# Low parts of split weights: a ScalarE copy with a negative sign and an accumulating DMA from GpSimd, in place of a VectorE subtraction

## The chip, the cores and the metric

The program runs on one core of a Trainium2 chip. The metric is the device time of one execution in microseconds; it is the median of three runs where several are given. The core has five engines, each with an instruction queue of its own that runs in order: TensorE (PE; its weight loads are PEld), VectorE (DVE), ScalarE (ACT), GpSimd (POOL) and SyncE (SP). SP issues most of the DMAs, GpSimd the rest; 16 DMA engines carry them.

## What is computed

Two blocks of a language model at sequence length 512 and width 1024, all in float32. The first has a convolution layer and a sliding-window layer, each followed by a feed-forward network; the second has compressed, selected and windowed attention beside a retention, then a gated merge. Nearly all of the arithmetic is in products of activations with weights:

```python
h = rmsnorm(x, norm_ffn[i])
x = x + (jax.nn.silu(h @ w_gate[i]) * (h @ w_up[i])) @ w_down[i]
...
y_b = (o_b * jax.nn.silu(z_r)) @ w_ret_o
merged = jax.nn.sigmoid(m_a) * y_a + jax.nn.sigmoid(m_b) * y_b
x = x + rms_norm(merged @ w_out, norm_post)
```

## The kernel before

Float32 products are made from three products in the format fp32r, which keeps fewer bits: each operand is split into a high part (the value rounded to fp32r) and a low part (what is left), and high x high, high x low and low x high are summed in PSUM. The names in the profile end in h and l for the two parts: `wh`, `wl` for weights, `gh`, `gl` and others for activations.

`weights` (L93) loads one weight tile of 128 x 1024 (512 KB; 896 columns in two thirds of the down projections, 512 in `w_nsa_o`, 1120 in `w_in_vg`) into `wr` by a DMA on SP (L102), copies it rounded into `wh` on ScalarE (L65, `copy`), and subtracts `wh` from `wr` into `wl` on VectorE (L75, `lo_of`). This happens 278 times. Only the first two tiles come in halves (`parts=2`), so that there are 280 copies and 280 subtractions. The buffers rotate: two `wr`, three `wh`, three `wl`. A load therefore waits until the tile two before it has been read for the last time, and a copy until TensorE is done with the tile three before it.

Two functions use the tiles. `proj` (L117) makes one 128 x 512 output from one tile: for each chunk of 128 rows, three matmuls (L111 to L113) of 512 columns, 24 for a tile of eight chunks, and the tile is free after that. `proj_tok` (L124) holds two tiles at once, of four chunks each, and goes through both for each block of 128 tokens (L133 to L135), so that both come free only in the last block.

The order of instructions on each engine is set when the program is built, by a scheduler that goes through the code in program order and puts each engine's instructions in a static queue. Semaphores do the rest. GpSimd's queue holds elementwise work too: the product `u` x `z` of each feed-forward column (L68), the squares and sums of the norms (L148, L157), clears of value tiles, and its own DMA issues.

Of the kernel before, what the change touches and what calls it, by code (L numbers as in the profile page):

```python
# [8 lines left out]
F32 = mybir.dt.float32  # L9
# [3 lines left out]
ALU = mybir.AluOpType  # L13
# [14 lines left out]
class Build:  # L28
# [65 lines left out]
    def weights(self, src, nk, nn, parts=1):  # L94

        nc, n = self.nc, nk * nn
        raw = self.wp.tile([128, 1120], F32, name=self.nm("wr"), tag="wr", bufs=self.wbufs["wr"])
        hi = self.wp.tile([128, WMAX], F32R, name=self.nm("wh"), tag="wh", bufs=self.wbufs["wh"])
        lo = self.wp.tile([128, WMAX], F32R, name=self.nm("wl"), tag="wl", bufs=self.wbufs["wl"])
        step = n // parts  # L100
        for s in (slice(a, a + step) for a in range(0, n, step)):
            nc.sync.dma_start(raw[:, s], src[:, s] if parts > 1 else src)  # L102
        for s in (slice(a, a + step) for a in range(0, n, step)):
            self.copy(hi[:, s], raw[:, s])
            self.lo_of(lo[:, s], raw[:, s], hi[:, s])
        v = lambda t: t[:, :n].rearrange("p (k c) -> p k c", k=nk)
        return v(hi), v(lo)

# [1017 lines left out]
```

## Time and profile before

| | us |
|---|---|
| median of three runs (1670.31 to 1672.84) | 1670.35 |
| the profiled execution's own time | 1670.48 |
| its span, first to last instruction | 1668.7 |
| TensorE busy in it | 1634.9 |
| VectorE busy | 1059.2 |
| ScalarE busy | 639.0 |
| GpSimd busy | 247.1 |
| SP's DMA queue, as busy time of all 16 DMA engines (27.3% of the span) | 455.6 |

The span is what the trace covers; the execution's own time is 1.8 us longer. TensorE's granted clock is full (a mean of 0.995) for nearly the whole span. Busy shares of TensorE overlap in the pipeline: a matmul of 512 columns shows 0.39 us, and the next one starts 0.23 us after it.

### The profile page before, as it was taken

What the parts mean: (1) busy time and instruction counts of PE and PEld (TensorE: products, weight loads), DVE (VectorE), ACT (ScalarE), POOL (GpSimd) and SP (SyncE); (2) the same over time, 40 slices, a digit from 0 to 9 for tenths busy, and PEclk for the clock granted to TensorE, in tenths of its full rate; (3) what the DMA queues carried; (4) which work ended last, traced back from release to release, by engine and by line L of the source; (5) the groups of instructions that cost most, each with busy time, mean ns of one, the idle gap of its engine ahead of it and who ended that gap; (6) DMA issues with size and microseconds to landing.
All of it is one profiled execution on the core that took longest, in us unless ns stands there. A gap on an engine that the chain in (4) does not pass through costs nothing.

```text
span 1668.7 us, 21221 instructions
## 1 busy us (share of the span) xinstructions
PE 1634.9 (98%) x8184; PEld 1374.2 (82%) x8184; DVE 1059.2 (63%) x1828; ACT 639.0 (38%) x1134; POOL 247.1 (15%) x220
## 2 busy tenths in 40 slices
PE   8999999999999999999999999998999999999997
PEld 6888888888888788888888888878788888888887
DVE  7776745444454979875434435588788977764443
ACT  5532333222333467633222223324465533333333
POOL 1111411002011600051100101351001000010010
PEclk9999999999999999999999999999999999999999
DMA  5323222322352422122332332332401122243342
GB/s 188 118 85 102 91 98 91 101 101 85 118 160 91 159 83 84 62 102 88 101 101 95 100 109 91 101 138 93 166 28 58 45 82 83 70 151 114 126 159 88
DMA packets 51557, 171.39 MB, mean 103 GB/s; under 512 B 6680, under 2 KB 6880, under 8 KB 51328
## 3 DMA queue, kind: packets, MB, share of 16 engines
q1 hardware_dynamic: 45504, 151.11, 27.3%
q0 software_dynamic: 5376, 18.82, 3.4%
q8 instruction: 64, 1.05, 0.2%
q14 instruction: 37, 0.30, 0.1%
q10 hardware_dynamic: 576, 0.11, 0.0%
HBM read 160.56 MB, written 11.81 MB: 103 GB/s over the span
## 4 chain that ended last, share of the span: by engine, by line
PE 82%; DVE 10%; issue 2%; ACT 2%; DMA 1%; POOL 1%; DVEq 0%; SPq 0%; ACTq 0%; POOLq 0%
PE pp L112 11%; PE pp L113 11%; PE pp L111 11%; PE lg L111 8%; PE lg L112 8%; PE lg L113 7%; PE tp L112 3%; PE tp L253 2%; PE tp L113 2%; PE tp L111 2%; DVE wl L75 2%; PE po L111 2%; PE po L112 2%; PE po L113 2%; PE pp L133 2%
## 5 line engine op out<-in xcount | busy, mean ns | idle before, releaser
L65 ACT ACTIVATE wh<-wr 128x1024 fp32r<-128x1024 f32 (+2 forms) x280 | 288.5, 1030 | 695.1 <-PE pp L112 228.0
L75 DVE TENSOR_TENSOR wl<-wr,wh 128x1024 fp32r<-128x1024 f32 (+2 forms) x280 | 388.7, 1389 | 55.5 <-ACT wh L65 52.3
L111 PE MATMUL pp<-gh,wh 128*128 128x512 f32 x880 | 348.0, 396 | 7.4 <-ACT wh L65 5.9
L113 PE MATMUL pp<-gh,wl 128*128 128x512 f32 x880 | 347.2, 395 | 0.6 <-DVE wl L75 0.6
L112 PE MATMUL pp<-gl,wh 128*128 128x512 f32 x880 | 346.7, 394 | 0.5 <-DVE gl L71 0.5
L111 PEld LDWEIGHTS pp<-gh,wh 128*128 128x128 f32 x880 | 166.7, 190 | 41.4 <-ACT wh L65 6.4
L113 PEld LDWEIGHTS pp<-gh,wl 128*128 128x128 f32 x880 | 166.4, 189 | 33.9 <-DVE wl L75 1.6
L112 PEld LDWEIGHTS pp<-gl,wh 128*128 128x128 f32 x880 | 166.6, 189 | 33.2 <-DVE gl L71 1.3
L111 PE MATMUL lg<-gh,wh 128*128 128x512 f32 x408 | 159.8, 392 | 0.0
L112 PE MATMUL lg<-gl,wh 128*128 128x512 f32 x408 | 159.1, 390 | 0.0
L113 PE MATMUL lg<-gh,wl 128*128 128x512 f32 x408 | 158.8, 389 | 0.0
L68 POOL TENSOR_TENSOR u<-u,z 128x512 f32<-128x512 f32 x44 | 64.8, 1472 | 549.7 <-DVE u L68 432.6
L68 DVE TENSOR_TENSOR u<-lg,Rf 128x512 f32<-128x512 f32 x44 | 30.4, 691 | 137.4 <-PE lg L113 137.3
L112 PEld LDWEIGHTS lg<-gl,wh 128*128 128x128 f32 x408 | 76.7, 188 | 16.5 <-issue 0.7
L111 PEld LDWEIGHTS lg<-gh,wh 128*128 128x128 f32 x408 | 76.6, 188 | 16.3 <-issue 0.5
L113 PEld LDWEIGHTS lg<-gh,wl 128*128 128x128 f32 x408 | 76.6, 188 | 16.1 <-issue 0.2
L112 PE MATMUL tp<-actl,wh 128*128 128x512 f32 x216 | 84.5, 391 | 0.9 <-DVE actl L75 0.9
L111 PE MATMUL tp<-acth,wh 128*128 128x512 f32 x216 | 84.1, 389 | 0.0
L113 PE MATMUL tp<-acth,wl 128*128 128x512 f32 x216 | 84.1, 389 | 0.0
L68 DVE TENSOR_TENSOR z<-pp,Rf 128x512 f32<-128x512 f32 x44 | 30.4, 691 | 69.5 <-PE pp L113 65.7
L504 DVE TENSOR_TENSOR x<-x,tp 128x512 f32<-128x512 f32 x36 | 24.6, 683 | 65.5 <-PE tp L113 65.5
L71 DVE SCALAR_TENSOR_TENSOR gl<-x,gains,gh 128x512 fp32r<-128x512 f32 x40 | 52.9, 1338 | 0.5 <-ACT gh L65 0.5
(422 smaller groups left out, 3088.9 us busy)
## 6 DMA issues: line engine op xcount, KB each, us to landing
wr<-in_w_gate_dram SPq DMA_DIRECT2D x44, 512.0 KB, 3.2
wr<-in_w_up_dram SPq DMA_DIRECT2D x44, 512.0 KB, 3.2
wr<-in_w_in_dram SPq DMA_DIRECT2D x44, 512.0 KB, 3.2
wr<-in_w_down_dram SPq DMA_DIRECT2D x32, 448.0 KB, 3.3
wr<-in_a_w_in_dram SPq DMA_DIRECT2D x18, 512.0 KB, 3.2
wr<-in_w_down_dram SPq DMA_DIRECT2D x16, 512.0 KB, 3.5
wr<-in_a_w_out_dram SPq DMA_DIRECT2D x8, 512.0 KB, 3.2
wr<-in_b_w_q_dram SPq DMA_DIRECT2D x8, 512.0 KB, 3.2
```

Of the source, the lines that this page charges most:

```text
L65: self.nc.scalar.activation(out, in_, AF.Copy, scale=scale)
L68: (eng or self.nc.vector).tensor_tensor(out, a, b, op=ALU.mult)
L71: (eng or self.nc.vector).scalar_tensor_tensor(out, a, s, b, op0=op0, op1=op1)
L75: self.nc.vector.tensor_tensor(out, x, hi.bitcast(F32), op=ALU.subtract)
L111: mm(ps, ah, bh, start=start, stop=False)
L112: mm(ps, ah, bl, start=False, stop=False)
L113: mm(ps, al, bh, start=False, stop=stop)
L133: mm(ps, a, wh, start=k == 0, stop=False)
L253: self.nc.tensor.transpose(ps[:, c:c + 128], src, self.ident)
L504: nc.vector.tensor_tensor(self.x[c], self.x[c], ps, op=ALU.add)
```

## The change

For every tile that is loaded whole, the subtraction on VectorE goes. ScalarE makes a second copy with scale -1 into `wl`, which leaves the rounded high part there with its sign turned, and a DMA issued by GpSimd then adds the raw tile to it in place (`accum_op=ALU.add`), reading `wr` and `wl` in SBUF and writing `wl`. The result is the same low part, not rounded again to fp32r. The two first tiles, in halves, keep the subtraction.

```diff
--- before.py
+++ after.py
@@ -102,7 +102,11 @@
             nc.sync.dma_start(raw[:, s], src[:, s] if parts > 1 else src)
         for s in (slice(a, a + step) for a in range(0, n, step)):
             self.copy(hi[:, s], raw[:, s])
-            self.lo_of(lo[:, s], raw[:, s], hi[:, s])
+            if parts > 1:
+                self.lo_of(lo[:, s], raw[:, s], hi[:, s])
+            else:
+                self.copy(lo[:, s], raw[:, s], -1.0)
+                nc.gpsimd.dma_start(lo[:, s].bitcast(F32), raw[:, s], accum_op=ALU.add)
         v = lambda t: t[:, :n].rearrange("p (k c) -> p k c", k=nk)
         return v(hi), v(lo)
```

With it, the `wr` buffer is read for the last time by the DMA, and no longer by VectorE: the next load into that buffer waits for the end of the DMA. TensorE's L113 waits for the DMA. SP's queue keeps its 316 entries in the same order but for small exchanges at two places. Lines after L104 have numbers higher by 4 in the changed kernel.

GpSimd's queue in the first feed-forward block, where before it holds only the products `u` x `z`:

```order
L68 TENSOR_TENSOR u_1825<-u_1825,z_1791 128x512
L68 TENSOR_TENSOR u_1897<-u_1897,z_1863 128x512
L68 TENSOR_TENSOR u_1969<-u_1969,z_1935 128x512
L68 TENSOR_TENSOR u_2041<-u_2041,z_2007 128x512
L68 TENSOR_TENSOR u_2113<-u_2113,z_2079 128x512
```

and now:

```order
L68 TENSOR_TENSOR u_1857<-u_1857,z_1822 128x512
L109 DMA wl_1941<-wr_1939 128x1024
L109 DMA wl_1976<-wr_1974 128x1024
L68 TENSOR_TENSOR u_1931<-u_1931,z_1896 128x512
L109 DMA wl_2015<-wr_2013 128x1024
L109 DMA wl_2050<-wr_2048 128x1024
L68 TENSOR_TENSOR u_2005<-u_2005,z_1970 128x512
L109 DMA wl_2089<-wr_2087 128x1024
L109 DMA wl_2124<-wr_2122 128x1024
```

Two issues stand between each product and the next; the product of one column stands ahead of the issue for the next column's gate tile.

ScalarE's queue at the same place, before (`wh` copies, the Silu of `z`, the high part of the product):

```order
L65 ACTIVATE wh_1940<-wr_1939 128x1024
L493 ACTIVATE z_1863<-z_1863 128x512
L65 ACTIVATE wh_1978<-wr_1977 128x1024
L65 ACTIVATE acth_1900<-u_1897 128x512
L65 ACTIVATE wh_2012<-wr_2011 128x1024
L493 ACTIVATE z_1935<-z_1935 128x512
```

and now:

```order
L65 ACTIVATE wh_1940<-wr_1939 128x1024
L65 ACTIVATE acth_1860<-u_1857 128x512
L65 ACTIVATE wl_1941<-wr_1939 128x1024
L65 ACTIVATE wh_1975<-wr_1974 128x1024
L65 ACTIVATE wl_1976<-wr_1974 128x1024
L497 ACTIVATE z_1896<-z_1896 128x512
L65 ACTIVATE wh_2014<-wr_2013 128x1024
L65 ACTIVATE wl_2015<-wr_2013 128x1024
```

Each `wh` copy has a `wl` copy of the same tile behind it, with at one place the high part of a product in between.

GpSimd's queue in the residual that feeds the first feed-forward norm, where it squares and sums the new `x` chunks, before:

```order
L148 TENSOR_TENSOR acc_1734<-x_81 128x512
L148 TENSOR_TENSOR sq_1736<-x_82 128x512
L157 TENSOR_TENSOR acc_1734<-acc_1734,sq_1736 128x512
L148 TENSOR_TENSOR sq_1739<-x_83 128x512
L157 TENSOR_TENSOR acc_1734<-acc_1734,sq_1739 128x512
```

and now:

```order
L109 DMA wl_1506<-wr_1504 128x1024
L152 TENSOR_TENSOR acc_1765<-x_81 128x512
L109 DMA wl_1539<-wr_1537 128x1024
L152 TENSOR_TENSOR sq_1767<-x_82 128x512
L161 TENSOR_TENSOR acc_1765<-acc_1765,sq_1767 128x512
L109 DMA wl_1572<-wr_1570 128x1024
L152 TENSOR_TENSOR sq_1770<-x_83 128x512
L161 TENSOR_TENSOR acc_1765<-acc_1765,sq_1770 128x512
```

One issue stands between each pair of a square and a sum and the next pair, so that the issue waits behind both, and behind what the square waits for.

## Rows read from the trace of the kernel before

**Rows 1.** The page: busy us, share and instructions of each engine
```profile
PE 1634.9 (98%) x8184; PEld 1374.2 (82%) x8184; DVE 1059.2 (63%) x1828; ACT 639.0 (38%) x1134; POOL 247.1 (15%) x220
```

**Rows 2.** The chain that ended last, its shares by line
```profile
by line: PE pp L112 11.4%; PE pp L113 11.4%; PE pp L111 11.3%; PE lg L111 7.6%; PE lg L112 7.6%; PE lg L113 7.5%; PE tp L112 2.5%; issue 2.5%; PE tp L253 2.5%; PE tp L113 2.4%; PE tp L111 2.4%; DVE wl L75 2.2%; PE po L111 2.2%; PE po L112 1
```

**Rows 3.** Groups by line: busy us, mean ns, idle before and its releasers
```profile
L75 DVE TENSOR_TENSOR wl<-wr,wh 128x1024 fp32r<-128x1024 f32 (+2 forms) x280 | 388.7, 1389 | 55.5 <-ACT wh L65 52.3
...
L65 ACT ACTIVATE wh<-wr 128x1024 fp32r<-128x1024 f32 (+2 forms) x280 | 288.5, 1030 | 695.1 <-PE pp L112 228.0 <-PE lg L112 196.4 <-PE tp L112 98.1
```

**Rows 4.** Timeline, first feed-forward block: start us, us, engine, line, operation
```profile
250.09 1.06 ACT L65 ACTIVATE wh<-wr 128x1024 fp32r<-128x1024 f32 x1 [2.44 <-PE pp L112]
...
251.18 1.22 DVE L75 TENSOR_TENSOR wl<-wr,wh 128x1024 fp32r<-128x1024 f32 x1 [0.22 <-ACT wh L65]
...
252.43 0.33 SPq L102 DMA_DIRECT2D wr<-in_w_up_dram  x1
...
255.53 1.06 ACT L65 ACTIVATE wh<-wr 128x1024 fp32r<-128x1024 f32 x1 [3.86 <-PE lg L112]
...
256.56 1.29 POOL L68 TENSOR_TENSOR u<-u,z 128x512 f32<-128x512 f32 x1 [9.59 <-DVE u L68]
256.62 2.32 DVE L75 TENSOR_TENSOR wl<-wr,wh 128x1024 fp32r<-128x1024 f32 x1 [0.23 <-ACT wh L65]
...
260.94 0.39 PE L111 MATMUL lg<-gh,wh 128*128 128x512 f32 x1
...
260.97 1.06 ACT L65 ACTIVATE wh<-wr 128x1024 fp32r<-128x1024 f32 x1 [2.44 <-PE pp L112]
```

**Rows 5.** DMA queues: packets, MB, share of 16 engines
```profile
q1 hardware_dynamic: 45504, 151.11, 27.3%
```

**Rows 6.** DMA issues: count, KB each, median us to landing
```profile
wr<-in_w_gate_dram SPq DMA_DIRECT2D x44, 512.0 KB, 3.2
...
wr<-in_w_down_dram SPq DMA_DIRECT2D x32, 448.0 KB, 3.3
...
band<-band POOLq DMA_DIRECT2D x1, 2304.0 KB, 13.8
...
wr<-in_w_nsa_o_dram SPq DMA_DIRECT2D x8, 256.0 KB, 2.8
...
xt<-xt POOLq DMA_DIRECT2D x8, 256.0 KB, 2.5
```

**Rows 7.** The same, issues from 541 to 549 us only
```profile
xres<-x POOLq DMA_DIRECT2D x2, 256.0 KB, 2.3
```

**Rows 8.** The same, issues from 552 to 560 us only
```profile
xres<-x POOLq DMA_DIRECT2D x2, 256.0 KB, 3.9
```

**Rows 9.** GpSimd from 541 to 560 us: one issue
```profile
542.26 0.59 POOL L514 DMA_DIRECT2D xres<-x  x1
```

**Rows 10.** ScalarE, 421 to 440 us, down projection of seven chunks
```profile
422.58 0.96 ACT L65 ACTIVATE wh<-wr 128x896 fp32r<-128x896 f32 x1 [3.80 <-PE po L112]
427.34 0.96 ACT L65 ACTIVATE wh<-wr 128x896 fp32r<-128x896 f32 x1 [3.80 <-PE tp L112]
```

**Rows 11.** ScalarE, 1154 to 1190 us, compression weights: first, one, last
```profile
1154.59 1.05 ACT L65 ACTIVATE wh<-wr 128x1024 fp32r<-128x1024 f32 x1
...
1167.68 1.06 ACT L65 ACTIVATE wh<-wr 128x1024 fp32r<-128x1024 f32 x1 [3.64 <-DMA wr<-in_w_in_dram]
...
1187.17 1.06 ACT L65 ACTIVATE wh<-wr 128x1024 fp32r<-128x1024 f32 x1 [0.19 <-DMA wr<-in_w_in_dram]
```

**Rows 12.** ScalarE, 1633 to 1638 us, output projection
```profile
1634.96 1.06 ACT L65 ACTIVATE wh<-wr 128x1024 fp32r<-128x1024 f32 x1 [0.78 <-PE pp L134]
1636.40 1.06 ACT L65 ACTIVATE wh<-wr 128x1024 fp32r<-128x1024 f32 x1 [0.38 <-PE pp L134]
```

**Rows 13.** Groups by line, GpSimd
```profile
L157 POOL TENSOR_TENSOR acc<-acc,sq 128x512 f32<-128x512 f32 x24 | 40.9, 1705 | 1.1
```

**Rows 14.** Windows, busy us of instructions with wl: PE, PEld, DVE
```profile
1122.00:1190.00 68.00, 36.38 (x109) 19.00 (x108) 19.81 (x15) 0.97 0.35 117
```

## The prediction

> **What bounds the kernel now.** I read the busy times first [rows 1]: TensorE is busy for 1634.9 us of 1668.7, so only 33.8 us of the span have no matmul at all. The chain that ended last, by line [rows 2], is matmul lines almost throughout; VectorE's low parts of weights (wl L75) hold 2.2% of it, 36.7 us. That is the most that this line's wait can be worth. The groups by line [rows 3] show the two steps of a weight tile: the copies on ScalarE cost 288.5 us in all, 1.03 us each, and before them ScalarE sits idle for 695.1 us, mostly until a matmul frees a buffer; the subtractions cost VectorE 388.7 us, 1.39 us each. Both steps run well ahead of TensorE.
>
> How far ahead, a stretch of the timeline shows [rows 4]. The copy into wh starts at 250.09 when a buffer comes free, the subtraction at 251.18, and the load for the tile after the next is issued at 252.43, as the subtraction ends. The next copies start at 255.53 and 260.97: one tile each 5.44 us, paced by the matmuls (a new tile begins at 260.94). The tile copied at 250.09 is the one used from 260.94, so its low part lies ready for more than 8 us. The two wr buffers give a second limit: two tiles take 10.88 us, and a buffer's own round (load 3.2 us [rows 6], copy 1.06, subtraction 1.22 to 2.32 [rows 4]) is 5.5 to 6.6 us. Here nothing waits for the weights.
>
> **What goes and what comes.** 276 of the 280 subtractions go, about 385 us of VectorE's 1059.2. ScalarE gets 276 copies of the size of wh's, 1.03 us each by [rows 3]: 284 us on 639.0 [rows 1], still 55% of the span. GpSimd gets 276 issues at 0.59 us each, the cost of a plain one [rows 9]: 163 us on 247.1. No engine becomes the bound by its sum. What decides is the wr buffer's round, which now holds a second copy and a whole DMA where a subtraction of 1.22 us was.
>
> **The DMA's time, D, from issue to landing.** No accumulating DMA and none from SBUF to SBUF stands in the trace, so I bound it. GpSimd's writes of 256 KB from SBUF landed in 2.3 us in one stretch [rows 7] and in 3.9 us ten microseconds later [rows 8]; another of its 256 KB copies has 2.5 us [rows 6]. SP's queue moved 151.11 MB in 27.3% of the span [rows 5], 455.6 us, which is 0.332 MB per us: 1.58 us for 512 KB and 0.79 for 256 KB. A plain copy of 512 KB from GpSimd is then 2.3 + 0.79 = 3.1 us. That is the lower bound, with the addition and the read of the old wl for nothing. If that second read goes through the same engines it adds 1.58: 4.7 us. Upper bound: GpSimd's slowest copy, 2304 KB in 13.8 us [rows 6], moves 0.17 MB per us; 512 KB twice at that rate is 6.1 us, and with the 1.5 us of the 2.3 that are not transfer 7.6 us. I take 4.7, since it rests on the quick 256 KB rows at the usual rate and the bytes that must be read.
>
> The Trainium skill speaks to the doubling (Collectives: The Full Stack, section on the bandwidth ceiling): an addition in the DMA path costs no time of its own but needs two source reads on the same ring, and a measured ratio of 1.93 to a plain copy is given. By it the transfer would be 3.05 us and D 4.6; by the plain-copy row alone D is 3.1 and the kernel would be some 1680 us. No run so far shows which holds.
>
> **Tiles of 512 KB in steady state.** The round is load 3.2, two copies 2.12, D 4.7, and 0.2 for hand-offs (at every second tile the issue also stands behind the product u x z, which ends at 257.85 [rows 4], 0.2 us after the second copy would): 10.2 us against 10.88. It hides, with 0.7 us to spare where 4.3 to 5.4 were. But one tile now needs 1.58 + 3.16 = 4.74 us of all 16 DMA engines out of 5.44, and the load into one buffer runs while the other buffer's addition does; each can lengthen the other by up to 1.58. I take 1.0: 11.2 us, an excess of 0.32 per two tiles, 0.16 per tile. Some 130 tiles (gate, up, large down, most of a_w_in and both out projections) have this pattern: 21 us.
>
> **Down projections of seven chunks.** The copies are 4.76 us apart [rows 10], 9.52 for two. The round is 3.3 [rows 6] + 2 x 0.96 + 4.3 (D less an eighth of its transfer) + 0.2 + 0.9 for sharing = 10.6: 0.55 for each of 32 tiles, 18 us.
>
> **Compression weights.** These tiles feed few matmuls, and the kernel already waits for loads here [rows 11]: from the first to the last copy nine steps of 3.62 us, with a wait for a raw tile among them. The new round of 10.2 us gives 5.1 per tile: 9 x 1.48 = 13 us.
>
> **Output projection.** proj_tok holds two of the three buffers, so that the second tile of the next group is copied only when the first of this group comes free, at 1634.96; the other comes free 1.44 us later, at 1636.40 [rows 12]. TensorE then has 1.44 us of the next group's first tile, so that the low part is needed about 3.1 us after 1634.96. Now it is there after 2.12 + 0.2 + 4.7 = 7.0: 3.9 us lost at three joints, 12 us. The eight other proj_tok calls have other tiles between them; each loses something from 0 to 3.9, I take 1.1: 9 us.
>
> **The rest.** In the merge, w_nsa_o tiles of 256 KB (load 2.8 [rows 6], copies 1.1, D 3.1, 0.2: 7.2) alternate with w_ret_o tiles (10.2); the mean of the rounds is 8.7 against 8.16 us of matmuls (5.44 and half of it): 0.5 in each of eight steps, 4 us. Where GpSimd squares and sums, the issue waits behind a square and a sum; a sum is 1.71 us [rows 13] and takes up more than the spare 0.7, and in three norms I count 5 us for both.
>
> **What comes back.** VectorE is relieved where it is on the chain: the subtractions are 19.8 us of the 68 from 1122 on [rows 14], the densest stretch. The 36.7 us of the chain and the 33.8 us without matmuls are ceilings; but in this stretch the subtraction's place is taken by the longer DMA, and ScalarE, which is in every softmax, gets a copy for each tile. I take 8 us.
>
> **Sum.** 21 + 18 + 13 + 12 + 9 + 4 + 5 - 8 = 74 us on the span of 1668.7: 1742.7, and with the 1.8 us outside it 1744.5. The profiled execution's own time, 1670.48, lies 0.13 above the median, so that 1744 stands for the median.
>
> **Rivals.** (1) The DMA is little slower than a plain copy, D from 3.1 to 3.9. The steady round is 8.6 to 9.4 us and hides with its sharing. Left are the joints: output projection 3 x 2.5 = 7, compression 6, the other calls 4, GpSimd's queue 3; less 8: +12, 1682. For it: the quick 256 KB row; against: the old wl must be read.
>
> (2) GpSimd's transfers start late beside a busy VectorE: the same 256 KB took 2.3 and 3.9 us [rows 7, 8]. D is then 6.3, the steady round with sharing 12.8: 0.96 x 130 = 125; seven chunks 1.25 x 32 = 40; the joints, compression and the rest grow by 1.6 us each time, from 43 to about 75. Less 8: +232, 1902. The Trainium skill has a rule for this (SBUF — State Buffer, section on its two separate sides): GpSimd cannot write descriptors while VectorE holds the shared port in a two-port mode. The page gives the plain two-input operation, which was VectorE's commonest, no such mode, so that by the rule D would stay at 4.7 in the feed-forward blocks; rows 7 and 8 do not say which operation held the transfer up.
>
> (3) The addition itself is slow, D near 7.6. The engines are then held so long that loads wait for all of their 1.58 us: the round is 14.7, 1.9 x 130 = 247; seven chunks 2 x 32 = 64; the rest about 90; less 8: +393, 2063.
>
> (4) Faster. If D is near 3.1 and the joints are covered by work that the scheduler moved there, the 36.7 us of low parts on the chain [rows 2] come back by half: -18 and +4, 1656. It decides from D under about 3 us.
>
> **Chances.** The forecast (1700 to 1800) 0.40, (1) 0.15, (2) 0.21, (3) 0.17, (4) 0.07. The forecast's own range is 1705 to 1795. To hold 8 in 10 the range leaves out (4) and the upper half of (3): 1676 to 2060. About 0.2%, 3.3 us, is what a measurement of this kernel can tell from no change. Faster by more has 0.07, within it 0.03 (a part of rival 1), slower 0.90.
>
> **What would show it.** In the changed profile: wl gone from VectorE but for four instructions, ScalarE near 920 us; a row of GpSimd's issues wl<-wr, whose time to landing is D: near 4.7 if the two reads are the cost, 3.1 to 3.9 for rival 1, over 6 for 2 and 3. The first start of L113 should wait for the DMA mainly in the seven-chunk down projections, the compression and the output projection. If the feed-forward copies still start each 5.44 us, sharing was mis-sized and the steady terms of 39 us go; if they start at 6.5 us or more, D was. I am wrong altogether if D is under 3 or over 8 us.

## The result, and the profile after

The changed kernel takes 1928.34 us (median of four runs, 1901.21 to 1952.99), the kernel before 1670.33: the ratio is 1.142, with a 95% interval from 1.135 to 1.150. (The two longest of the four runs are left out of the ratio, which is why it is below 1928/1670.) The profiled execution took 1915.94 us with a span of 1913.8. The forecast was 1744: the direction was right, the size was not. The measured time lies inside the stated range of 1676 to 2060, but outside the forecast's own of 1705 to 1795. On the span 245 us came on where I had summed up 74.

The page of the changed kernel: busy times, GpSimd's DMA queue (packets, MB, share of 16 engines), the chain that ended last, by engine and by line, groups of instructions, and two rows of DMA issues (KB each, median us to landing).

```profile
PE 1711.9 (89%) x8184; PEld 1401.3 (73%) x8184; DVE 686.1 (36%) x1552; ACT 878.1 (46%) x1410; POOL 453.5 (24%) x496
...
q0 software_dynamic: 45120, 159.44, 42.1%
...
DMA 46%; PE 31%; issue 12%; ACT 7%; DVE 2%; POOL 1%; SPq 0%; ACTq 0%; POOLq 0%; DVEq 0%
DMA wl<-wr 24%; DMA wr<-in_w_gate_dram 6%; DMA wr<-in_w_down_dram 4%; ACT wl L65 4%; PE pp L117 4%; PE pp L116 4%; PE pp L115 4%; DMA wr<-in_w_in_dram 3%; DMA wr<-in_w_up_dram 3%; PE tp L257 2%; DMA wr<-in_a_w_in_dram 2%; PE po L115 2%; PE lg L117 1%; PE lg L115 1%; PE po L116 1%
...
L65 ACT ACTIVATE wh<-wr 128x1024 fp32r<-128x1024 f32 (+2 forms) x280 | 287.6, 1027 | 826.9 <-DMA wr<-in_w_down_dram 168.0
L109 POOL DMA_DIRECT2D wl<-wr x276 | 238.8, 865 | 1189.8 <-ACT wl L65 1005.4
L117 PE MATMUL pp<-gh,wl 128*128 128x512 f32 x880 | 356.3, 405 | 33.4 <-DMA wl<-wr 33.3
...
wl<-wr POOLq DMA_DIRECT2D x234, 512.0 KB, 5.0
wr<-in_w_gate_dram SPq DMA_DIRECT2D x44, 512.0 KB, 4.2
```

The chain is no longer made of matmuls [rows 2]: its largest link is the loop of a raw buffer, addition (24%), load, copy. ScalarE's copies into wh waited for matmuls before [rows 3]; now they wait for loads, and the matmuls of L117 (L113 before) wait for the low part. VectorE lost 373 us of work [rows 1], and no gain from it can be seen. The addition's D is 5.0 us in the median, near my 4.7; but the loads, 3.2 before [rows 6], now take 4.2.

That median hides two patterns. The first, from 555 to 576 us, as a timeline (start us, us, engine, line, operation, idle before and its releaser):

```profile
562.08 0.86 POOL L109 DMA_DIRECT2D wl<-wr  x1 [6.09 <-ACT wl L65]
562.18 0.51 PE L117 MATMUL pp<-gh,wl 128*128 128x512 f32 x1 [1.34 <-DMA wl<-wr]
562.19 0.33 SPq L102 DMA_DIRECT2D wr<-in_w_gate_dram  x1
...
566.35 1.06 ACT L65 ACTIVATE wh<-wr 128x1024 fp32r<-128x1024 f32 x1 [4.57 <-DMA wr<-in_w_gate_dram]
...
568.65 0.86 POOL L109 DMA_DIRECT2D wl<-wr  x1 [4.39 <-ACT wl L65]
568.76 0.50 PE L117 MATMUL lg<-gh,wl 128*128 128x512 f32 x1 [0.81 <-DMA wl<-wr]
568.77 0.33 SPq L102 DMA_DIRECT2D wr<-in_w_up_dram  x1
```

Each addition (562.08) is issued 0.1 us ahead of the load for the other buffer (562.19), and so again at 568.65 and 568.77, with two tiles to a round: a buffer is loaded at 562.2 and again at 575.4, 13.2 us later. What the DMA engines do in the 3.3 us that follow the two issues shows in the packets of the queues from 562 to 565.3 us (the last two rows: the issues of this window, us to landing):

```profile
q1 hardware_dynamic: 119, 0.48, 60.4%
q0 software_dynamic: 2, 0.01, 1.2%
...
wl<-wr POOLq DMA_DIRECT2D x1, 512.0 KB, 6.6
wr<-in_w_gate_dram SPq DMA_DIRECT2D x1, 512.0 KB, 4.1
```

The load (q1) moves all but its last packets and the addition (q0), although issued first, next to nothing: the addition does not share with the load, it stands behind it. D is 6.6 there, and TensorE gets a tile each 6.6 us instead of 5.44.

The second pattern, 296 to 313 us:

```profile
296.79 0.87 POOL L109 DMA_DIRECT2D wl<-wr  x1 [4.83 <-ACT wl L65]
...
299.21 0.86 POOL L109 DMA_DIRECT2D wl<-wr  x1 [1.56 <-ACT wl L65]
301.27 0.33 SPq L102 DMA_DIRECT2D wr<-in_w_gate_dram  x1
...
304.23 0.33 SPq L102 DMA_DIRECT2D wr<-in_w_up_dram  x1
...
307.81 0.87 POOL L109 DMA_DIRECT2D wl<-wr  x1 [4.74 <-DMA wr<-in_w_up_dram]
...
310.24 0.86 POOL L109 DMA_DIRECT2D wl<-wr  x1 [1.55 <-ACT wl L65]
312.31 0.33 SPq L102 DMA_DIRECT2D wr<-in_w_down_dram  x1
```

Two additions follow each other in 2.4 us, then both loads; the two additions land in 4.7 us (their median). The round is 312.31 - 301.27 = 11.04 us, almost the 11.2 that I had forecast for everywhere. Here it is the load that waits: it is issued at 301.27, and from 302 to 303.2 us the engines start 61 packets of the additions and none of its own. In both patterns the transfer whose packets come first goes through first. Below, "lockstep" is the first pattern and "pairs" the second.

### The profile page after: what moved, and what is told of

It reads as the page before. It is cut to its first block, busy times and chain, and to the rows that moved or that the text cites. A ratio compares the mean times of both kernels' runs of the same rounds, so it can differ in the third digit from the quotient of the medians.

```text
span 1913.8 us, 21841 instructions
## 1 busy us (share of the span) xinstructions
PE 1711.9 (89%) x8184; PEld 1401.3 (73%) x8184; DVE 686.1 (36%) x1552; ACT 878.1 (46%) x1410; POOL 453.5 (24%) x496
## 3 DMA queue, kind: packets, MB, share of 16 engines
q0 software_dynamic: 45120, 159.44, 42.1%
## 4 chain that ended last, share of the span: by engine, by line
DMA 46%; PE 31%; issue 12%; ACT 7%; DVE 2%; POOL 1%; SPq 0%; ACTq 0%; POOLq 0%; DVEq 0%
DMA wl<-wr 24%; DMA wr<-in_w_gate_dram 6%; DMA wr<-in_w_down_dram 4%; ACT wl L65 4%; PE pp L117 4%; PE pp L116 4%; PE pp L115 4%; DMA wr<-in_w_in_dram 3%; DMA wr<-in_w_up_dram 3%; PE tp L257 2%; DMA wr<-in_a_w_in_dram 2%; PE po L115 2%; PE lg L117 1%; PE lg L115 1%; PE po L116 1%
## 5 line engine op out<-in xcount | busy, mean ns | idle before, releaser
L109 POOL DMA_DIRECT2D wl<-wr x276 | 238.8, 865 | 1189.8 <-ACT wl L65 1005.4
L117 PE MATMUL pp<-gh,wl 128*128 128x512 f32 x880 | 356.3, 405 | 33.4 <-DMA wl<-wr 33.3
L115 PE MATMUL pp<-gh,wh 128*128 128x512 f32 x880 | 354.9, 404 | 20.8 <-ACT wh L65 14.8
L116 PE MATMUL pp<-gl,wh 128*128 128x512 f32 x880 | 352.5, 401 | 0.9 <-DVE gl L71 0.9
L65 ACT ACTIVATE wl<-wr 128x1024 fp32r<-128x1024 f32 (+3 forms) x276 | 281.3, 1019 | 0.6 <-PE pp L117 0.6
L117 PEld LDWEIGHTS pp<-gh,wl 128*128 128x128 f32 x880 | 169.7, 193 | 80.1 <-DMA wl<-wr 46.8
L117 PE MATMUL lg<-gh,wl 128*128 128x512 f32 x408 | 164.0, 402 | 12.0 <-DMA wl<-wr 11.9
L117 PEld LDWEIGHTS lg<-gh,wl 128*128 128x128 f32 x408 | 77.7, 191 | 35.7 <-DMA wl<-wr 19.1
L75 DVE TENSOR_TENSOR actl<-u,acth 128x512 fp32r<-128x512 f32 x36 | 24.9, 693 | 208.5 <-ACT acth L65 208.5
L117 PE MATMUL tp<-acth,wl 128*128 128x512 f32 x216 | 87.0, 403 | 7.5 <-DMA wl<-wr 7.5
L71 DVE SCALAR_TENSOR_TENSOR gl<-x,gains,gh 128x512 fp32r<-128x512 f32 x40 | 39.0, 989 | 95.4 <-ACT gh L65 95.4
```

The source lines that it names most:

```text
L65: self.nc.scalar.activation(out, in_, AF.Copy, scale=scale)
L71: (eng or self.nc.vector).scalar_tensor_tensor(out, a, s, b, op0=op0, op1=op1)
L75: self.nc.vector.tensor_tensor(out, x, hi.bitcast(F32), op=ALU.subtract)
L109: nc.gpsimd.dma_start(lo[:, s].bitcast(F32), raw[:, s], accum_op=ALU.add)
L115: mm(ps, ah, bh, start=start, stop=False)
L116: mm(ps, ah, bl, start=False, stop=False)
```

## The experiments

How long each tile is late is worked out from the traces: the time from the first matmul of one tile to that of the next, less the same time in the kernel before, summed over the tiles that are waited for (in the order of before). In us, with the count of tiles; "changed" is the changed kernel, e1 to e12 the experiments, "mem, kv" the tiles of w_mem_k, w_mem_v, w_kv_k and w_kv_v, "layer a" those of a_w_in and a_w_out:

```
tiles      count  changed       e1       e2       e3       e4       e6       e8      e10      e11      e12
gate, up      88     62.0     11.3     11.6      0.2     12.3     20.5     71.1      5.5     70.0     21.0
down          48     33.6     -2.1      0.7     -2.1     -1.9      4.5     42.8      0.1     21.9      3.7
layer a       28     17.7      0.7      6.9     -0.2      3.2     10.2      3.1     15.0      1.0      6.5
mem, kv       12     33.5     10.9      5.2     -1.9      9.3      4.8      7.7     23.1      8.4      4.8
w_in          44     46.2     14.7     29.1      7.6     17.5      3.4      6.8     44.4      5.4      6.9
cmp_w1         8     21.9     13.0     17.7      1.7     10.9     18.0     -1.6     18.6     -1.9      0.3
w_out          8     17.5     10.0     28.3      0.8     10.4     16.0     -0.0     19.8     -0.0      0.1
w_nsa_o        8      7.9      0.1      0.7      0.0      0.8      0.9     -0.6      9.3      0.0      1.4
the rest      34      1.9      2.9      6.2      0.3     -0.9     -1.8     -0.0      4.4     -0.1      6.3
sum          278    242.3     61.5    106.3      6.5     61.8     76.6    129.2    140.1    104.7     50.9
```

A negative number is a tile that came sooner than before, or other work that the static queues put elsewhere.

My theory, called S in the expectations: loads and additions pass one behind the other, and a raw buffer's round cannot hold both. The rivals: the second read of the addition is not what costs (L), the 16 engines are simply full, or ScalarE's second copy holds up the chain.

**e1, a plain copy in place of the addition.**

```diff
-                nc.gpsimd.dma_start(lo[:, s].bitcast(F32), raw[:, s], accum_op=ALU.add)
+                nc.gpsimd.dma_start(lo[:, s].bitcast(F32), raw[:, s])
```

> The DMA from GpSimd only copies the raw weights over wl and adds nothing (so the low parts hold the whole weight; what is left out is the subtraction of the high part). The waits, the queues and ScalarE's second copy are those of the changed kernel. Theory S (the transfers of loads and additions do not share the 16 engines but pass one behind the other, and the raw buffer's round cannot hold both): a transfer with one read takes about 1.3 to 1.6 us instead of 2.6, D alone 3.1 to 3.4, behind a load about 5; the round is at most 3.2 + 2.1 + 5 + 0.2 = 10.5 of 10.88 us, so the steady loss goes: 1690 to 1735 us. Theory L (what costs is that a DMA from GpSimd starts late and stands in the wait chain, however little it moves): D stays above 4.5, 1850 us or more.

1733.62 us, a ratio of 1.039 (1.037 to 1.041). Its queue of GpSimd and its issues:

```profile
q0 software_dynamic: 42560, 159.44, 23.4%
...
L109 POOL DMA_DIRECT2D wl<-wr x276 | 152.6, 553 | 924.4 <-ACT wl L65 832.1
...
wl<-wr POOLq DMA_DIRECT2D x234, 512.0 KB, 3.1
wr<-in_w_gate_dram SPq DMA_DIRECT2D x44, 512.0 KB, 3.2
```

D is 3.1 us, my lower bound to the digit, and the loads are back at 3.2. Down, layer a and the merge (w_nsa_o) lose nothing more. L falls: the waits and queues are the same and three quarters of the loss are gone. What is left, 61 us, sits where stages meet; 11.6 of it lies in one feed-forward group, which is told below.

**e2, the addition reads HBM, so that wr is free after the two copies.**

```diff
-                nc.gpsimd.dma_start(lo[:, s].bitcast(F32), raw[:, s], accum_op=ALU.add)
+                nc.gpsimd.dma_start(lo[:, s], src.bitcast(F32R), accum_op=ALU.add)
```

> The accumulating DMA reads the raw weights from HBM instead of from wr, so that a raw buffer is free once ScalarE has made its two copies: round 3.2 + 2.1 = 5.3 to 7 us instead of 10 to 13.5. The number and size of the additions stay. Theory S: the raw buffer's round was what held the kernel; D may stay at 4.5 to 7, but a wl buffer has 10.85 us from its copy to its use, of which 2.1 + 7 + 0.2 = 9.3 are used; left are the joints (output projection, compression, the ends of stages): 1700 to 1760 us. Rival (the additions themselves keep the 16 engines too long, whoever waits): the same number of bytes must still be added, over 1860 us.

1781.67 us, 1.067 (1.064 to 1.069), somewhat over the range of S.

```profile
q0 software_dynamic: 45120, 159.44, 48.1%
...
wr<-in_w_gate_dram SPq DMA_DIRECT2D x44, 512.0 KB, 5.2
...
wl<-in_w_gate_dram POOLq DMA_DIRECT2D x44, 512.0 KB, 7.7
```

This is the clearest reading of the study: loads take 5.2 us and additions 7.7, both longer than in the changed kernel, and yet gate, up and down lose 12 us instead of 96. Neither the engines' load nor D itself cost there; the raw buffer that was held for D did. The long D costs where a low part is needed soon: 28 us in the output projection (17.5 in the changed kernel), which I had not counted in. (Both sides are named as fp32r here; the queue moves the same 159.44 MB.)

**e3, the ScalarE part alone.**

```diff
-                nc.gpsimd.dma_start(lo[:, s].bitcast(F32), raw[:, s], accum_op=ALU.add)
+                nc.vector.tensor_tensor(lo[:, s], raw[:, s], lo[:, s].bitcast(F32), op=ALU.add)
```

> ScalarE's negated copy stays, and VectorE adds the raw weights (no DMA): the ScalarE part of the change alone. All theories that blame the DMA: within 10 us of the kernel before, 1665 to 1682. Rival (the second copy on ScalarE, in front of the copies of act and z, holds up the chain): 1720 us or more.

1677.3 us, 1.0044 (1.0029 to 1.0059). The 276 copies cost some 7 us by themselves. ScalarE's work is not the cause; that the order of its queue passes a late load on is told below.

**e4, half of each tile by the DMA.**

```diff
-                self.copy(lo[:, s], raw[:, s], -1.0)
-                nc.gpsimd.dma_start(lo[:, s].bitcast(F32), raw[:, s], accum_op=ALU.add)
+                h = slice(0, n // 2)
+                self.copy(lo[:, h], raw[:, h], -1.0)
+                nc.gpsimd.dma_start(lo[:, h].bitcast(F32), raw[:, h], accum_op=ALU.add)
+                h = slice(n // 2, n)
+                self.lo_of(lo[:, h], raw[:, h], hi[:, h])
```

> Only the left half of each tile goes by ScalarE's negated copy and the accumulating DMA; VectorE subtracts the right half as before. Theory S: D alone is 1.43 + 1.3 + 0.35 = 3.1 us, behind a load 5; the round is 3.2 + 1.6 + 5 + 0.2 = 10 at most, under 10.88: 1690 to 1730 us, a third or less of the loss although half of the bytes stay. Rival (each added byte costs its share, wherever it lies): half of the 258 us stays, about 1800. Theory L (a late start of each DMA, whatever its size): over 1850.

1734.16 us, 1.039 (1.037 to 1.040), just over the range of S: a quarter of the loss for half of the bytes. D is 3.3 us for 256 KB. True additions that are short enough for the round cost about what the plain copies of e1 cost: every row of the table is within 4 us.

**e5 and e6, a third raw buffer.** There is no room in SBUF for one, so some was given up elsewhere first (e5), and then used (e6).

```diff
-WMAX = 1152
+WMAX = 1120
-        self.sm = pool("sm", 4)
+        self.sm = pool("sm", 3)
-    def square_sum(self, chunks, n=512, first=False, gain2=None, tags=("sa", "s")):
+    def square_sum(self, chunks, n=512, first=False, gain2=None, tags=("s", "s")):
-        self.const("pad", [128, 88])
...
-        self.wbufs = dict(wr=2, wh=3, wl=3)
+        self.wbufs = dict(wr=3, wh=3, wl=3)
```

(In the slots' counts sa=1 goes and k3=2 becomes k3=1. The last pair of lines is e6 alone.)

> The changed kernel with some SBUF given up elsewhere (one buffer less for small tiles and the last keys, the sums of squares in the slots of the squares, wh and wl 1120 wide), and nothing put in its place: the control of the next run. All theories: the time of the changed kernel, 1900 to 1955 us.

> The control with a third raw buffer in the space given up. Theory S (a raw buffer's round of load, two copies and addition cannot hold a load and an addition that pass one behind the other): three buffers may take 16.3 us for their round, and 4.5 + 2.1 + 7 + 0.2 = 13.8 fits even where every addition waits behind a load; the loss of the gate, up, down and a-layer tiles (113 us by the traces) goes but for 20, the joints stay: 1730 to 1790 us. Rival (the 16 engines are the bound, or additions are too slow whoever waits): within 40 us of the control.

1953.15 us for e5 (1.169, 1.162 to 1.176), 25 us above the changed kernel's median and at the upper end of its four runs; 1750.58 for e6 (1.0485, 1.0469 to 1.0500).

```profile
wl<-wr POOLq DMA_DIRECT2D x234, 512.0 KB, 5.8
wr<-in_w_gate_dram SPq DMA_DIRECT2D x44, 512.0 KB, 5.1
```

As in e2, additions and loads are slower than in the changed kernel, and the buffer that makes room for them takes back 203 us against the control and 178 against the changed kernel. For that part the engines are not the bound.

**e7, no loads.** In front of the tiles one raw tile is loaded; only the first two tiles, which go in two parts, have a load of their own.

```diff
-        raw = self.wp.tile([128, 1120], F32, name=self.nm("wr"), tag="wr", bufs=self.wbufs["wr"])
+        raw = self.raw0 if parts == 1 else self.wp.tile([128, 1120], F32, name=self.nm("wr"), tag="wr", bufs=1)
...
-        for s in (slice(a, a + step) for a in range(0, n, step)):
+        for s in (slice(a, a + step) for a in range(0, n if parts > 1 else 0, step)):
             nc.sync.dma_start(raw[:, s], src[:, s] if parts > 1 else src)
```

> All weight tiles but the first two are made from one raw tile that is loaded once (left out: the other 278 loads; all tiles hold the same weights). The copies, the additions and their waits stay; no load runs beside an addition and no raw buffer is waited for. Theory S: D is 4.4 to 5.0 us throughout, never 6 to 8 except behind another addition; steady loss nil, the joints cost what a D of 4.5 costs there: 1690 to 1730 us. Rival (additions are held up by VectorE's or ScalarE's work, or by GpSimd): D keeps its tail of 6 to 8 us.

1691.54 us, 1.0133 (1.0117 to 1.0148).

```profile
PE 1642.6 (97%) x8184; PEld 1377.9 (81%) x8184; DVE 694.8 (41%) x1552; ACT 885.9 (52%) x1410; POOL 451.9 (27%) x496
...
wl<-wr POOLq DMA_DIRECT2D x234, 512.0 KB, 4.4
```

D is 4.4 us, and nine in ten additions land within 5.5; in the changed kernel about one in four takes 6 us or more. VectorE, ScalarE and GpSimd do here what they do there, so none of them is what holds an addition up. The 21 us left are a balance, worked out as in the table. Where a low part is needed at once, a D of 4.4 costs 11.4 us in the output projection, 8.7 in the compression, some 8 in layer a and 5.7 in gate and up; the other tiles come 13 us sooner, since no load is waited for.

**e8 and e10, each half of the tiles alone.** e10 has the condition without its "not".

```diff
-            if parts > 1:
+            if parts > 1 or not (src.tensor.name in FFNW):
```

(FFNW holds the names of w_gate, w_up and w_down.)

> Only the tiles of w_gate, w_up and w_down (136 of 276) go by ScalarE's negated copy and the accumulating DMA; the others are subtracted by VectorE as before. The steady term by itself. By the traces these tiles hold 62 + 34 = 96 of the 242 us: if the terms add, 1766 us (1745 to 1785). My prediction's terms for them (21 x 88/130 + 18 = 32) give 1702. If the slow pattern is started by the joints of other stages and only then keeps itself up, less than 96 remains: 1700 to 1740.

> The converse of the kernel with the DMA in the feed-forward tiles only: the other 140 tiles go by the negated copy and the accumulating DMA, w_gate, w_up and w_down are subtracted by VectorE as before. If the losses add, 1928 - 112 = 1816 us (1790 to 1840); by the table of the changed kernel's trace these tiles hold 147 of 242 us. My prediction's terms for them (74 - 39 + 9 for the attention projections) give 1714.

1782.38 us for e8 (1.0685, 1.062 to 1.075) and 1813.81 for e10 (1.0868, 1.084 to 1.090): 112 and 145 us over before, together 257 of the 258. The sums of the profiled executions are 129 and 140 beside 242. The runs of the changed kernel lie 52 us apart, so as far as this can tell the losses add. In e8 the feed-forward tiles lose 114 us in the profiled execution, where my terms gave them some 32, so that the lockstep does not need the other stages to start it.

**e9 and e11, one delay.** e8 again, with one addition in each of the six groups held back. For e9 twelve small products of GpSimd stood ahead of it:

> The kernel with the DMA in the feed-forward tiles only (1782 us), and on GpSimd twelve small products ahead of the addition of the second up tile of each of the six groups: one delay of some 3 us, six times in all. In the traces a feed-forward stretch is in one of two patterns: each tile 1.1 to 1.3 us late (every addition issued together with the other buffer's load), or pairs of additions close behind each other and 0 to 0.3 us late. Theory: the pattern keeps itself up, so one delay turns the late pattern into the other; after each delay the tiles are 0 to 0.3 us late on average, gate and up lose 45 us or less instead of 71: 1745 to 1765 us with the delays' own cost. Rival (what runs beside a stretch makes it late): tiles are again 1.1 to 1.3 us late right after the delay, 1782 to 1800.

It took 1798.22 us (1.0743, 1.0702 to 1.0785), but tested nothing: the products depend on nothing, and the scheduler put all 72 of them between 2 and 45 us of the program. It is e8 once more, and shows how far its times lie apart (1772 to 1813 in the eight runs of the two). In e11 the delay works on the tile itself and has to stay:

```diff
                 self.copy(lo[:, s], raw[:, s], -1.0)
+                for _ in range(2 if nudge else 0):
+                    nc.gpsimd.tensor_scalar(lo[:, s], lo[:, s].bitcast(F32), 1.0, None, op0=ALU.mult)
                 nc.gpsimd.dma_start(lo[:, s].bitcast(F32), raw[:, s], accum_op=ALU.add)
```

> The DMA in the feed-forward tiles only, and for the fourth up tile of each of the six groups GpSimd multiplies the negated high part twice by one, in place, ahead of the addition, so that this one addition is held back by the two products (some 3 to 5 us); the scheduler cannot move them, as it did with the small products of the run before. Theory (a pattern that keeps itself up): where the tiles before were each 1.1 to 1.3 us late, the delayed tile costs 3 to 5 us and those behind it are 0 to 0.3 us late until the group's end; gate and up lose 71 us or less although six delays of 3 to 5 us are added: 1765 to 1800 us. Rival (the stretch makes them late): 1.1 to 1.3 us late again within two tiles, and the delays on top: 1800 to 1830 us.

1773.51 us (1.0628, 1.0594 to 1.0661). First e8, from 834 us on, then e11, from 832 us on, in the second block's first group:

```profile
834.12 0.85 POOL L110 DMA_DIRECT2D wl<-wr  x1 [4.66 <-ACT wl L66]
834.23 0.33 SPq L103 DMA_DIRECT2D wr<-in_w_gate_dram  x1
...
840.72 0.86 POOL L110 DMA_DIRECT2D wl<-wr  x1 [3.17 <-ACT wl L66]
840.84 0.33 SPq L103 DMA_DIRECT2D wr<-in_w_up_dram  x1
```

```profile
832.10 0.87 POOL L112 DMA_DIRECT2D wl<-wr  x1 [2.40 <-ACT wl L66]
832.21 0.33 SPq L103 DMA_DIRECT2D wr<-in_w_up_dram  x1
...
838.72 5.63 POOL L111 TENSOR_SCALAR wl<-wl 128x1024 fp32r<-128x1024 f32 x2 [5.75 <-ACT wl L66]
839.02 0.33 SPq L103 DMA_DIRECT2D wr<-in_w_gate_dram  x1
...
844.65 0.89 POOL L112 DMA_DIRECT2D wl<-wr  x1 [0.30 <-POOL wl L111]
...
846.50 1.17 POOL L112 DMA_DIRECT2D wl<-wr  x1
...
849.18 0.33 SPq L103 DMA_DIRECT2D wr<-in_w_up_dram  x1
852.06 0.33 SPq L103 DMA_DIRECT2D wr<-in_w_gate_dram  x1
```

e8 stays in lockstep, an addition and a load 0.1 us apart every 6.6 us. In e11 the lockstep runs as well ahead of the delay (832.10 and 832.21). The one held addition (844.65) is followed by the other buffer's (846.50), then come both loads: the pairs have begun. How late each gate and up tile of this group is, worked out as in the table, before and behind the delayed one (the lockstep shows no lateness at first, since TensorE still has tiles that were made ready earlier):

```
e8   0.0  0.0 -0.1 -0.0  0.0 -0.0  0.1  1.3  1.1  1.2  1.2  1.3  4.1  0.0  0.9  1.4
e11  0.0 -0.0 -0.1 -0.0  0.0  0.0  0.0  0.4  7.0  0.0 -0.0  0.0 -0.0  0.0 -0.0  0.0
```

Over all six groups the tiles behind the delayed one are late by 2.7 us in e11 and 32 in e8, and down by 22 instead of 43. The six delays themselves show as 3.8 to 8.6 us each, 42 together, and even so e11 is no slower than e8. So what runs beside a stretch does not by itself put it into the lockstep; it matters how the transfers stood before.

**e12, three raw buffers and the two worst joints back on VectorE.** e6, with the tiles of cmp_w1 and w_out subtracted as before.

> The kernel with three raw buffers (1751 us), with the 16 tiles of the compression and of the output projection subtracted by VectorE as before; 260 tiles go by the DMA. In the trace of the kernel with three raw buffers these two stages hold 18 + 16 = 34 of its 77 us. Theory (there the low part is needed sooner than a DMA can land, whatever the raw buffers): 1717 us (1708 to 1726). Rival (the loads of these tiles, lengthened by additions elsewhere, are what is late there): 1735 us or more.

1723.12 us (1.0325, 1.0307 to 1.0343), within the range: 27 of e6's 80 us. The table has 0.3 and 0.1 in the two stages; the other rows are 8 us above those of e6 in sum. Of the versions whose low parts all hold the right values and that use the DMA, none comes nearer to the kernel before than these 3.2%.

## Why the prediction was wrong

**The step that failed first** is in the part on tiles of 512 KB: "each can lengthen the other by up to 1.58. I take 1.0: 11.2 us, an excess of 0.32 per two tiles". That round is the one of the pairs, 11.04 us. In the lockstep the addition stands behind the whole load: D goes from 4.4 (e7) to 6.6, the load from 3.2 to 4.1, and the round is 4.1 + 2.1 + 6.6 + hand-offs, 13.2. Where it stands the excess is 1.2 per tile, not 0.16. Both patterns exist in the same code, and a delay turns one into the other (e11). The two bounds together, 2 x 1.58 on 10.2, would have given 13.4, near what the lockstep takes. I took 1.0 of these 3.2 without a row for it, and had not asked at what moment of the round the two transfers meet: the landing of one addition issues a load just when the other addition is issued. By the prediction's own sign, tiles at 6.5 us or more, D would have been mis-sized; but D alone was right, and it was the sharing that was too small.

By my own terms, in us, measured from the table of the changed kernel (gate, up, layer a and the 13.5 of the two large down groups in the first row; the other four down groups in the second; all are net sums, and what VectorE gave back cannot be told apart in them):

| term | predicted | measured |
| --- | --- | --- |
| 512 KB tiles in steady state | 21 | 62.0 + 17.7 + 13.5 = 93 |
| seven-chunk down projections | 18 | 20 |
| compression weights | 13 | 22 |
| output projection | 12 | 17.5 |
| other token projections (measured: mem, kv) | 9 | 33.5 |
| merge (its w_in and w_nsa_o) | 4 | 15.2 + 7.9 = 23 |
| other w_in, all the rest | 5 | 31 + 2 = 33 |
| back from VectorE | -8 | none seen |
| sum | 74 | 242 |

The 93 of the first row are not all lockstep's 1.2 per tile. In the profiled execution 48 of the 276 additions are issued within 0.3 us of a load. Of the 62.0 of gate and up, 22.0 lie in 16 tiles that are 0.9 to 2.0 us late, and 35.5 in seven that are over 2 us late. e2 and e6 say that most of this hangs on the raw buffer too, but it reaches TensorE by other ways. One of them is ScalarE's queue, which the prediction does not have: a copy that waits for a load holds up the activation behind it. The second tile of the first down group shows it:

```profile
329.40 1.06 ACT L65 ACTIVATE wh<-wr 128x1024 fp32r<-128x1024 f32 x1 [6.27 <-DMA wr<-in_w_down_dram]
...
331.31 0.61 ACT L65 ACTIVATE acth<-u 128x512 fp32r<-128x512 f32 x1
...
331.97 0.50 PE L115 MATMUL tp<-acth,wh 128*128 128x512 f32 x1 [2.37 <-ACT acth L65]
```

TensorE waits for the high part of an activation, acth, that stands behind the two copies of a weight tile, and these behind a load. Such waits for acth, gh and tph are 21.7 us in the changed kernel and 1.5 before. The seven-chunk term is right in size. It is not a proof of its working: two of the four groups lose most at the second and third tile, in this way.

The row of the token projections does not hold just what its term meant either: w_mem_k and w_kv_k, which are no proj_tok calls, lose 20.0 of the 33.5, and five of the eight calls (w_in_vg and w_in_vr) lose nothing.

**The second step** is the joints: "The eight other proj_tok calls ... I take 1.1: 9 us". With a D of 3.1 rival 1 put all joints at some 20 us; e1, with exactly that D, loses 61. Some places were right (output projection 10, compression 13) and others were missing: the feed-forward group behind the memory projections loses 11.6 us in e1, which is all that gate and up lose there, and 24.5 of the changed kernel's 62. In e2, e4, e6 and e12 this group loses 10 to 12 us as well. In e1 the largest part of it is this:

```profile
465.60 0.54 POOL L335 DMA_DIRECT2D band<-band  x1 [1.98 <-DMA band<-s]
...
466.50 0.33 SPq L102 DMA_DIRECT2D wr<-in_w_gate_dram  x1
...
479.24 0.80 PE L115 MATMUL pp<-gh,wh 128*128 128x512 f32 x1 [7.00 <-ACT wh L65]
```

The copy of 2304 KB from band to band [rows 6] is issued 0.9 us ahead of a load, and the load lands after 11.6 us. TensorE waits 7.0 us for a high part, and 5.6 at the same place of the changed kernel. In the kernel before a load behind the same copy takes 10.8 us, and no matmul waits: the tiles were far enough ahead. The change used up that lead, and I had looked for joints only where two buffers are held.

In the output projection I had counted three joints of 3.9 us. In the changed kernel TensorE waits 1.9, 1.9 and 2.6 us there, and 6.3 in the first pair of tiles, which I had not counted, so that 12 against 17.5 is nearer than its working was. The first pair, with loads that stand behind additions:

```profile
1851.06 1.06 ACT L65 ACTIVATE wh<-wr 128x1024 fp32r<-128x1024 f32 x1 [9.37 <-DMA wr<-in_w_out_dram]
...
1851.91 0.58 PE L139 MATMUL pp<-wl,mgh 128*128 128x256 f32 x1 [6.34 <-DMA wl<-wr]
```

**A term was missing: the clock.** TensorE's mean granted clock is 0.964, where it was 0.995. Where TensorE waits for long, the matmuls after the wait are slower. The stretch of the compression (rows: window, span, busy us of PE, PEld, DVE, ACT and POOL, granted clock, DMA share, GB/s):

```profile
1317.00:1375.00 58.00, 31.71 (x155) 25.46 (x153) 17.08 (x54) 28.45 (x45) 10.15 (x12) 0.76 0.73 166
...
560.00:590.00 30.00, 24.58 (x103) 18.74 (x102) 4.66 (x7) 11.88 (x14) 8.06 (x8) 1.00 0.70 154
```

TensorE was busy there for 31.7 of 58 us, and the clock fell to 0.76 [rows 14 has 0.97 for the stretch before]. By the two means TensorE stood at 1.2 instead of 2.4 GHz for 2 x 0.036 x 1913.8 = 138 us of the span, and for 17 before. Intervals between the starts of matmuls of 1.7 to 2.3 times their usual length add up to some 50 us over the usual in the changed kernel and 16 before. So an estimated 35 of the 242 us are matmuls at the lower clock; they lie inside the terms of the table. The lockstep's waits of 1.2 us in each tile leave the clock at 1.00 (second row).

**What held.** D: bounds 3.1 to 7.6, taken 4.7; alone it is 4.4 (e7), and a plain copy takes 3.1 (e1). An addition's transfer is thus about twice a copy's, as a second read would make it; the runs do not tell that from an addition that is slow by itself. The packets of GpSimd's queue took 46.0% of 1691.1 us in e7 and 23.4% of 1730.1 in e1; less the other transfers of this queue (3.3% of 1675.6 in e3) that is 723 against 350 us, a ratio of 2.07. The Trainium skill (Collectives: The Full Stack, section on the bandwidth ceiling) has 1.93 for an addition's two source reads against a copy's one, measured on collectives; the trace, on one core, is near it. ScalarE is at 878 us where I said 920; the copies into wl start 0.1 us ahead of the end of those into wh (566.35 + 1.06 and 567.31), so that their records overlap, which makes some 28 of these 42 us. An issue cost GpSimd 0.87 us and not 0.59 (0.55 for the plain copies of e1); GpSimd holds 1% of the chain.

**The rivals.** Rival 2 came nearest to the time (1902), by a D that is close to the lockstep's (6.3), but for a cause that is not there: transfers late beside a busy VectorE. Without loads D loses its long tail, while VectorE is as busy as in the changed kernel (694.8 and 686.1 us). The rule of the Trainium skill that I weighed (SBUF — State Buffer, section on its two separate sides), by which VectorE's commonest operation would not hold up GpSimd's transfers, agrees with that. Rival 3's slow addition falls with e7, where D is 4.4, and rival 1's cheap one too. Rival 4 falls with e1, where D is 3.1 and the kernel is still 63 us slower than before.

**What stays open.** Why a load's packets pass ahead of an addition that was issued 0.1 us earlier is not shown; the first packet of an addition comes 1.43 us behind its issue even with nothing else under way, and the load's came 0.98 us behind its own, at 563.17, so that they were there first. How much of the 242 us goes by each of the ways (low parts that come late, activations behind copies, lead that is gone) is not told apart: e2 and e6 take the raw buffer's hold away and most of all of them with it. That the differences between runs of the changed kernel (1901 to 1953 us) are the lockstep's share in each is likely from e8, e9 and e11, but was not counted, since each kernel has one profile.

## What to carry to other kernels

A step that moves from an engine to a DMA lengthens the hold on the buffer it reads, so write out that buffer's round with the other transfers at the worst moment, not at an even share: loop lengths that just fit can lock two transfers against each other for many rounds. If the DMA must be, give its source a buffer of its own or read it from elsewhere (e6 and e2 took back 178 and 147 us of the changed kernel's time, with longer transfers). Look for low slack wherever tiles with few matmuls follow each other, and beside every large transfer that was hidden by a lead which the change uses up. See what else stands in the queue of an engine that now waits for a load. And the clock that falls in a long wait is paid on top.

## What the runs showed of the hardware

A transfer of GpSimd and one of SP that were issued 0.1 us apart did not share the 16 engines by turns: from 562 to 565.3 us 119 packets of the load went and 2 of the addition. The other way round, from 302 to 303.2 us, 61 packets of additions went and none of the load. A load issued 0.9 us behind a copy of 2304 KB landed after 11.6 us instead of 3.2 (e1). Two timings of the same loop stand in one execution: 6.6 and 5.5 us per tile. An accumulating DMA of 512 KB costs GpSimd 0.87 us to issue and a plain one 0.55.
